# Sixteen batched matmuls on one core: from eight loads and turns of four stores to nine loads, eight stores, seven loads, eight stores

## The chip, the cores and the metric

The kernel runs on one core of a Trainium2 chip. The metric is device time in microseconds (us) of one execution; the time given is the median of several runs. One further execution was profiled, and all rows of the profile come from it.

## The reference

For each of 16 batches, x (768 x 512) transposed times y (768 x 1024), all in float32:

```python
batch, m, k, n = 16, 512, 768, 1024
# x: (batch, k, m), y: (batch, k, n)
np.einsum('bkm,bkn->bmn', x, y).astype(np.float32)
```

The inputs are drawn from a normal distribution. A batch reads 1.5 MB of x and 3 MB of y and writes 2 MB.

## The kernel before

Batches are the unit of everything. A batch b is loaded as float32 into `xs[b % 2]` and `ys[b % 2]` (one DMA for x, one for y), cast to bfloat16 by VectorE (DVE) into half b % 2 of `xb` and `yb`, multiplied by TensorE (PE), copied from PSUM by ScalarE (ACT) into `ob[b % 5]`, and stored by one DMA. There are NO = 5 output buffers `ob`.

PE works through a batch in two groups g of 48 / 2 = 24 matmuls each: a group is two of the four row blocks `mo` and fills one half of PSUM, `ps[g]`. It waits for a token of `room` before each group (L152); ACT returns a token after each copy (L176). So PE can be at most two groups ahead of the copies. PE counts finished groups in `groups` (L162), two per batch. Before a batch it waits for the casts (`ready`, L148, passed on from `cast` by GpSimd).

ACT takes the batches in order. Before batch b's copies, for b of 5 and up, it waits until the store that last used the buffer, of batch b - 5, has landed (`so`, L170).

DVE casts x of batch b after PE has finished batch b - 2 (L129: `groups` at least 2(b - 1)) and x has landed, then y when y has landed. The last batch's y is cast in two parts.

All DMAs, loads and stores, are issued by one engine, SyncE (SP), in the order of its program, into one queue. Each issue first waits on SP:

- `load(b)` (L104): x of batch b waits until x of batch b - 2 has been cast, y until y of b - 2 has been cast, since they share a buffer.
- `store(b)` (L95): waits until batch b + 1 has left PE (`groups` at least 2(b + 2), L99), which implies that batch b's copies are done, since the last group of b + 1 needed their `room`. The stores of batches 14 and 15 wait for the copies themselves (`outs`).

An instruction of SP that waits holds back all that follow it. The order of the program is made at L113 to L120 from FIRST = 8 and TURN = 4: loads 0 to 7, stores 0 to 3, loads 8 to 11, stores 4 to 7, loads 12 to 15, stores 8 to 14. The store of batch 15 follows at L188, after SP has waited for the stores of batches 11 to 13 (L182) and for the other engines.

Of the kernel before, what the change touches and what calls it, by code (L numbers as in the profile page):

```python
# [3 lines left out]

# [2 lines left out]

# [8 lines left out]
def kernel(  # L16
# [11 lines left out]
    B, K, M = x.shape  # L28
# [9 lines left out]
    y_v = y.rearrange("b (p ko) n -> b p ko n", ko=KT)  # L38
    o_v = out.rearrange("b (p mo) n -> b p mo n", mo=MT)

    FIRST = 8
    TURN = 4
    NO = 5
    KH = KT // 2

# [24 lines left out]
    def wide_dma(key, dst, src, dram_rows, load):  # L70


        if key not in made:
            made[key] = nc.sync.dma_start(dst, src)
            return made[key]
        pat = mybir.BassSymbolicTensorAccessPattern
        widen = lambda a: a.rearrange("(q r) k m -> q (r k m)", r=dram_rows)
        plain = lambda a: a.rearrange("p k m -> p (k m)")
        s, d = (widen(src), plain(dst)) if load else (plain(src), widen(dst))
        return nc.sync.add_instruction(_copy.replace(  # L80
            made[key].ins, name=nc.get_next_instruction_name(),
            ins=(pat(ap=s.ap, dtype=s.dtype, bass_ap=s, is_dma=False),),
            outs=(pat(ap=d.ap, dtype=d.dtype, bass_ap=d, is_dma=False),),
            sync_info=None, ant_dge_precooked=False))


    def parts(b):
        return 2 if b in (15,) else 1
# [2 lines left out]
    nx = [sum(1 + parts(a) for a in range(b)) + 1 for b in range(B)]  # L91

    def store(b):  # L95


        if b < B - 2:
            nc.sync.wait_ge(groups, 2 * (b + 2))  # L99
        else:  # L100
            nc.sync.wait_ge(outs, b - (B - 3))
        nc.sync.dma_start(o_v[b], ob[b % NO][:]).then_inc(so[b % NO], 16)

    def load(b):  # L104
        i = b % 2
        if b >= 2:
            nc.sync.wait_ge(cast, nx[b - 2])
        wide_dma("x", xs[i][:], x_v[b], 4, True).then_inc(sx[i], 16)
        if b >= 2:
            nc.sync.wait_ge(cast, nx[b - 2] + parts(b - 2))  # L110
        wide_dma("y", ys[i][:], y_v[b], 2, True).then_inc(sy[i], 16)

    for b in range(B):  # L113
        load(b)
        if b + 1 >= FIRST and (b + 1 - FIRST) % TURN == 0:
            a = b + 1 - FIRST
            for c in range(a, a + TURN):
                store(c)
    for b in range(B - FIRST + TURN, B - 1):
        store(b)  # L120


    for _ in range(60):
# [95 lines left out]
```

## Time and profile before

| what | us |
|---|---|
| median of 3 runs (lowest to highest) | 260.62 (260.34 to 261.06) |
| the profiled execution's own time | 260.58 |
| its span, first to last record | 258.8 |
| PE busy, of the span | 181.6 (70%) |
| DVE busy | 82.0 (32%) |
| ACT busy | 60.9 (24%) |
| issue to landing, median: load of x / of y / store | 20.1 / 18.6 / 27.2 |

The page's second part cuts the span into 40 slices of 6.5 us; each digit is the busy share of a slice in tenths. Its third part gives for each DMA queue the packets, the MB and the time that the packets took, as a share of 16 DMA engines over the span. Its fifth part lists groups of instructions: line, engine and operation, output and input, count, then busy time, the mean in ns of one, and the engine's idle time just before them with what ended most of it. In the timeline a row gives start, duration, engine (SPq is SP's queue of DMA issues; its duration is the issue, not the transfer), line, operation, count, and in brackets the idle time before and what ended it.

PE ran in these stretches: 18.9 to 62.7, 62.9 to 73.4, 73.8 to 84.4, 99.2 to 123.0, 126.5 to 150.3, 162.6 to 185.5, 189.8 to 212.4 and 226.0 to 249.6 us.

### The profile page before, as it was taken

What the parts mean: (1) busy time and instruction counts of PE and PEld (TensorE: products, weight loads), DVE (VectorE), ACT (ScalarE), POOL (GpSimd) and SP (SyncE); (2) the same over time, 40 slices, a digit from 0 to 9 for tenths busy, and PEclk for the clock granted to TensorE, in tenths of its full rate; (3) what the DMA queues carried; (4) which work ended last, traced back from release to release, by engine and by line L of the source; (5) the groups of instructions that cost most, each with busy time, mean ns of one, the idle gap of its engine ahead of it and who ended that gap; (6) DMA issues with size and microseconds to landing.
All of it is one profiled execution on the core that took longest, in us unless ns stands there. A gap on an engine that the chain in (4) does not pass through costs nothing. (4 is left out here: it accounts for less than half of the span.)

```text
span 258.8 us, 2506 instructions
## 1 busy us (share of the span) xinstructions
PE 181.6 (70%) x768; PEld 89.3 (34%) x768; DVE 82.0 (32%) x33; ACT 60.9 (24%) x33; POOL 0.2 (0%) x4
## 2 busy tenths in 40 slices
PE   0009999999999006999499920899669980099950
PEld 0004555554545002454145500355325530035520
DVE  0261645527164350011734525002255262300000
ACT  1000442234220005222214002324402200413430
POOL 0000000000000000000000000000000000000000
PEclk9999999999999855899779985699979995569995
DMA  7999989899999999999999989999899999999987
GB/s 273 424 475 410 471 380 479 372 479 395 456 410 441 387 418 430 466 446 418 433 433 425 471 352 443 420 461 479 372 479 403 448 410 390 433 438 420 436 357 324
DMA packets 4514, 109.07 MB, mean 421 GB/s; under 512 B 768, under 2 KB 768, under 8 KB 768
## 3 DMA queue, kind: packets, MB, share of 16 engines
q1 hardware_dynamic: 4512, 109.05, 98.6%
q14 instruction: 2, 0.02, 0.0%
HBM read 75.50 MB, written 33.55 MB: 421 GB/s over the span
## 5 line engine op out<-in xcount | busy, mean ns | idle before, releaser
L157 PE MATMUL ps<-yb,xb 128*128 x768 | 181.6, 402 | 68.0 <-PEq L152 68.0
L157 PEld LDWEIGHTS ps<-yb,xb 128*128 x768 | 89.3, 116 | 159.8 <-issue 89.8
L173 ACT COPY ob<-ps 128x2048 f32<-128x2048 f32 x32 | 59.6, 1872 | 185.3 <-PE ps L157 125.2
L135 DVE CAST yb<-ys 128x6144 bf16<-128x6144 f32 (+1 forms) x17 | 53.8, 3172 | 77.8 <-DMA ys<-in_y_dram 77.8
L131 DVE CAST xb<-xs 128x3072 bf16<-128x3072 f32 x16 | 28.2, 1761 | 62.5 <-DMA xs<-in_x_dram 48.7
L173 ACT ACT_TABLE_LOAD x1 | 1.3, 1283 | 5.3 <-issue 5.3
L203 POOL MEMSET const-bfloat16-1.0<- 128x1 bf16 x1 | 0.1, 103 | 0.0
L203 POOL MEMSET const-uint8-127<- 128x1 uint8 x1 | 0.1, 102 | 0.0
L203 POOL MEMSET const-float32-0.0<- 128x1 f32 x1 | 0.1, 100 | 0.2 <-issue 0.2
L203 POOL MEMSET const-float32-1.0<- 128x1 f32 x1 | 0.1, 99 | 0.0
## 6 DMA issues: line engine op xcount, KB each, us to landing
ys<-in_y_dram SPq DMA_DIRECT2D x16, 3072.0 KB, 18.6
out_dram<-ob SPq DMA_DIRECT2D x16, 2048.0 KB, 27.2
xs<-in_x_dram SPq DMA_DIRECT2D x16, 1536.0 KB, 20.1
```

The source lines that it names most:

```text
L131: nc.vector.tensor_copy(xb[:, i], xs[i][:]).then_inc(cast, 1)
L135: nc.vector.tensor_copy(yb[:, i, ks], ys[i][:, ks]).then_inc(cast, 1)
L157: mm = nc.tensor.matmul(ps[g][:, m, nt], x_w[:, bass.ds(s, 1), kt, mo], yb[:, bass.ds(s, 1), kt, nt * NF:(nt + 1) * NF], start=(kt == 0), ...
L173: cp = nc.scalar.copy(ob[b % NO][:, g * HB:(g + 1) * HB].rearrange("p m (t f) -> p m t f", f=NF), ps[g][:])
L203: nc = _bacc.Bacc("TRN2", target_bir_lowering=False, num_devices=1)
```

## The change

The two constants and the loop that made SP's order are replaced by a list of turns, each a number of loads and a number of stores. The order is now: loads 0 to 8, stores 0 to 7, loads 9 to 15, stores 8 to 14 (the last turn asks for eight stores; seven remain, and the store of batch 15 is issued at the end as before). `load`, `store`, their waits, the five output buffers and all other engines' programs are unchanged.

```diff
-    FIRST = 8
-    TURN = 4
+    TURNS = [(9, 8), (7, 8)]
     NO = 5
...
-    for b in range(B):
-        load(b)
-        if b + 1 >= FIRST and (b + 1 - FIRST) % TURN == 0:
-            a = b + 1 - FIRST
-            for c in range(a, a + TURN):
-                store(c)
-    for b in range(B - FIRST + TURN, B - 1):
-        store(b)
+    loads, stores = iter(range(B)), iter(range(B - 1))
+    for nl, ns in TURNS:
+        for b in islice(loads, nl):
+            load(b)
+        for b in islice(stores, ns):
+            store(b)
```

More of the change, by code (lines that the diff above doesn't have):

```diff
@@ L6 @@
 from contextlib import ExitStack
+from itertools import islice
 import concourse.bass as bass
```

## The prediction

> **What bounds the kernel now.** I read the page first: parts 2 and 3 for which resource is full, part 5 for who waits.
>
> ```profile
> DMA  7999989899999999999999989999899999999987
> q1 hardware_dynamic: 4512, 109.05, 98.6%
> L157 PE MATMUL ps<-yb,xb 128*128 x768 | 181.6, 402 | 68.0 <-PEq L152 68.0
> L173 ACT COPY ob<-ps 128x2048 f32<-128x2048 f32 x32 | 59.6, 1872 | 185.3 <-PE ps L157 125.2
> ```
>
> The one DMA queue is busy 98.6% of the span, PE 70%, ACT 24%. So the transfers set the time, and PE's 68.0 us of waiting for `room` cost nothing so long as the queue has something to move. [...] So next I read the timeline, where a cast begins when its load has landed and a copy that waited for an output buffer begins when that store has landed.
>
> ```profile
> 69.96 3.36 DVE L135 CAST yb<-ys 128x6144 bf16<-128x6144 f32 x1 [5.48 <-DMA ys<-in_y_dram]
> 73.71 1.76 DVE L131 CAST xb<-xs 128x3072 bf16<-128x3072 f32 x1 [0.39 <-DMA xs<-in_x_dram]
> 80.94 3.36 DVE L135 CAST yb<-ys 128x6144 bf16<-128x6144 f32 x1 [5.47 <-DMA ys<-in_y_dram]
> ...
> 92.12 3.36 DVE L135 CAST yb<-ys 128x6144 bf16<-128x6144 f32 x1 [5.66 <-DMA ys<-in_y_dram]
> ...
> 97.00 3.64 ACT L173 COPY ob<-ps 128x2048 f32<-128x2048 f32 x2 [21.69 <-DMA out_dram<-ob]
> ...
> 99.19 23.85 PE L157 MATMUL ps<-yb,xb 128*128 x96 [14.79 <-PEq L152]
> ...
> 107.59 1.87 ACT L173 COPY ob<-ps 128x2048 f32<-128x2048 f32 x1 [6.95 <-PE ps L157]
> 112.71 1.87 ACT L173 COPY ob<-ps 128x2048 f32<-128x2048 f32 x1 [3.26 <-PE ps L157]
> 115.34 1.76 DVE L131 CAST xb<-xs 128x3072 bf16<-128x3072 f32 x1 [19.86 <-DMA xs<-in_x_dram]
> 117.95 1.87 ACT L173 COPY ob<-ps 128x2048 f32<-128x2048 f32 x1 [3.37 <-PE ps L157]
> 123.07 1.87 ACT L173 COPY ob<-ps 128x2048 f32<-128x2048 f32 x1 [3.26 <-PE ps L157]
> ```
>
> Three things are to be seen. A load of one batch takes 10.98 us (y of batch 5 at 69.96, of 6 at 80.94), its x part 3.75 (69.96 to 73.71). The transfers land in the order of issue: y of batch 7 at 92.12, store 0 at 97.00 (4.88 later), then stores 1 to 3 and x of batch 8 by 115.34; 18.34 less 3.75 is three stores, 4.86 each. The same reading after y of batch 11 (copies at 160.43, cast at 178.65) gives 4.82; I use 4.84. And the first copy of batch 5 waits for store 0, because buffer 0 of five is still full; PE, with both PSUM halves occupied, stands still until it comes.
>
> The chain of waits names the end, and the timeline what precedes it:
>
> ```profile
> 218.85 3.43 DVE L135 CAST yb<-ys 128x3072 bf16<-128x3072 f32 x2 [4.69 <-DMA ys<-in_y_dram]
> 223.74 3.63 ACT L173 COPY ob<-ps 128x2048 f32<-128x2048 f32 x2 [19.83 <-DMA out_dram<-ob]
> 225.98 23.60 PE L157 MATMUL ps<-yb,xb 128*128 x96 [13.61 <-PEq L152]
> 249.61 1.87 ACT L173 COPY ob<-ps 128x2048 f32<-128x2048 f32 x1 [3.26 <-PE ps L157]
> 251.67 0.33 SPq L188 DMA_DIRECT2D out_dram<-ob  x1
> ```
>
> Store 8 lands at 223.74 and frees batch 13's copies; then come batches 14 and 15 on PE, the last copy, the last store. That is 35.1 us from store 8's landing to the end of the span, with all other stores beside it.
>
> [...] This trace: the last store, issued when the queue was all but empty, took 6.3 us to landing (the minimum of the landing times), 1.5 over the 4.84 of a store in a full queue; I use 6.3. [...] Here the first group of matmuls after a pause takes 8.40, 8.41, 7.41, 7.15 and 8.15 us (PE's start to the first copy after it), a later one 5.12 or 5.24.
>
> **The change part by part.**
>
> *Up to y of batch 7* nothing differs: the same loads, waits and landings.
>
> *Load 8 ahead of store 0.* It waits for the casts of batch 6, as before, so it is in the queue in time (those casts end at 75.5 and 84.3, while y of batch 7 is under way to 92). Its 10.98 us are moved, not added: y of batch 8 lands at 80.94 + 2 x 10.98 = 102.9, and store 0 at 107.8 instead of 97.0. PE idles 10.8 us longer after batch 5 (from 84.4); in itself that is free.
>
> *Stores 0 to 7 in one run.* Store b waits on SP until batch b+1 has left PE (L99). Stores 0 to 4 need batch 5, done at 84.4: they are issued at once. Stores 5, 6 and 7 need batches 6, 7 and 8, which PE can't begin before store 0 has landed. Before, store 7 had no such trouble: its four stores came after load 11 with batch 8 done at 140.0, and y of batch 11 landed at 155.5, so the queue was full. Now count from store 0's landing at 107.8, with the steps of the trace:
> - copies of batch 5 begin, PE restarts 2.18 later (97.00 to 99.18 there);
> - batch 6 takes 7.90 (mean of the five first groups) + 5.12, done at +15.2; batch 7 5.24 + 5.12, done at +25.6; batch 8 likewise, done at +35.9. Batch 8's casts begin when batch 6 is done and take 5.2, so they lie beside batch 7's 10.4; without that cover batch 8 would come later.
> - The queue moves stores 1 to 5 by +24.2 (5 x 4.84). Store 5 is issued at +15.2, in time.
> - Store 6 is issued at +25.6, lands 6.3 later at +31.9; in a full queue it would land at +29.0. Lost: 2.8.
> - Store 7 is issued at +35.9, lands at +42.2, where 7 x 4.84 = 33.9 would be the full queue. Lost: 8.3 in all, so 5.5 more.
>
> Nothing else can use these gaps: loads 9 to 15 stand behind store 7 in SP's own order, though their buffers are long free.
>
> *Loads 9 to 15* follow store 7 back to back: load 9 needs casts of batch 7, load 10 those of batch 8 (done near 128, store 7 issued at 143.7). PE restarts after y of batch 9, and at 10.4 a batch against 10.98 for a load it keeps up; copies of batches 9 to 12 need stores 4 to 7, landed. I cost this stretch at nothing beyond the shift. The bytes and transfers before y of batch 15 are the same 16 loads and 8 stores, so it lands 8.3 later: 227.2.
>
> *The end* is as before: batch 13's copies wait for store 8, and the 35.1 us follow.
>
> *Two turns fewer* from stores back to loads and on again: a first store after a load takes 4.88 against 4.84, so two turns are worth about 0.1 gained, and I drop it.
>
> **Sum.** 8.3 us on the profiled execution's own 260.58 (span 258.8, 1.8 around it), which is the median of the runs (260.62) but for 0.04: 268.9 us.
>
> Unknown sizes, bounded from both sides: the first group after a pause, 7.15 to 8.41, moves the gap by -0.8 to +0.5; the same ramp recurs at the end, where 8.15 is in the 260.58, so -1.0 to +0.3 there. A restart from an empty queue: at least the 0.9 between the last issue (251.67) and the first bytes after it, in windows of half a microsecond, at most the 2.5 of the first load (issued 0.95, cast at 7.18, less 3.75), against my 1.5: -0.6 to +1.0. These rarely all go one way: 267.5 to 270.5.
>
> **The rivals.**
>
> *Longer stop (chance 8%).* PE's pause is now some 26 us instead of 15[...]. For: [...] the queue's restart price rests on one store. Against: five restarts in the trace all lie within 1.3 us, after pauses of 3.4 to 14.8, and the very first group of the kernel, cold, took 7.5. It would give 270.5 to 273; with a clock that stays at half through batches 6 to 8, some 20 us more, which I hold for 1%.
>
> *Partly hidden (chance 5%).* the gap ahead of store 6 closes, because PE comes back sooner than I say or the stores drain more slowly, so that only store 7's remains: 8.3 - 2.8 = 5.5, 266.1. Against: store 6's wait for batch 7 follows from rates that repeat within 0.1.
>
> *Not slower (chance 3%).* One mechanism: the turns between reading and writing. The old order has five of them, the new three. If a turn cost 4.2 us or more, two fewer would pay for the gap: 260.6, and below it beyond that. The place to see it is the first transfer after each turn; there 4.88 stands against 4.84, and x of batch 8 and 12 show no loss either. That leaves the price near 0.05, and this rival nearly nothing to live on but a turn cost hidden in my averages.
>
> *The change not done:* the order of SP's instructions shows load 9 (batch 8) ahead of eight stores and seven loads behind them; nothing else moves. No chance left for it.
>
> **How the numbers follow.** Forecast 84%, longer stop 8%, partly hidden 5%, not slower 3%. The likeliest: 268.9. The range 267.4 to 270.8 holds the forecast's case and the near edge of the longer stop, leaving out somewhat under 2 in 10. All but the last case are slower by over 0.3% (0.8 us, about what a measurement of this kernel can tell from no change): slower 0.97, within 0.3% 0.01, faster 0.02.
>
> **What would show it.** In the profile after: copies of batch 5 near 107.8; PE without a pause over batches 6 to 8 (144 matmuls from about 110); stores issued singly near 123, 133.4 and 143.7; the DMA row with a dip between 131 and 146 and nowhere else; x of batch 9 cast near 153.7; y of batch 15 near 227.2; SP's waits on PE longer by the ones on stores 5 to 7. It is wrong if store 7 is issued before about 136 (then there is no gap), if the queue stays full between 131 and 146, or if a second gap opens among loads 9 to 15.

## The result and the profile after

| | before | after |
|---|---|---|
| median, us (lowest to highest) | 260.53 (260.34 to 261.06, 4 runs) | 269.90 (269.74 to 270.49, 4 runs) |
| profiled execution: time / span | 260.58 / 258.8 | 270.49 / 268.7 |
| share of the one DMA queue | 98.6% | 95.4% |

The ratio after to before is 1.0361, with a 95% interval of 1.0338 to 1.0383: 9.4 us slower. The profiled execution of after was the longest of its four, so its own difference is 9.9.

The page of the changed kernel, parts 2, 3 and 5:

```profile
DMA  7999999999999998999474999989989989999996
q1 hardware_dynamic: 4512, 109.05, 95.4%
L154 PE MATMUL ps<-yb,xb 128*128 x768 | 175.9, 393 | 82.2 <-PEq L149 82.2
```

The bytes are the same and the queue's share has fallen by 3.2 points of a longer span. The missing share lies in one place: slices 20 to 22 of the row, 4, 7 and 4 tenths. A slice is 6.7 us, so this is 127 to 148 us. PE idles more in total (82.2 us against 68.0), but that is no proof of anything, since it idled before without harm.

The timeline of the changed kernel at the run of eight stores and after it (start, duration, engine, line, what; SPq is the issue on SP; the three single stores are numbers 5, 6 and 7; ... stands for rows left out):

```profile
107.85 3.64 ACT L170 COPY ob<-ps 128x2048 f32<-128x2048 f32 x2 [32.49 <-DMA out_dram<-ob]
110.03 34.15 PE L154 MATMUL ps<-yb,xb 128*128 x144 [25.59 <-PEq L149]
...
118.38 1.87 ACT L170 COPY ob<-ps 128x2048 f32<-128x2048 f32 x1 [6.89 <-PE ps L154]
123.50 0.33 SPq L101 DMA_DIRECT2D out_dram<-ob  x1
...
133.85 0.33 SPq L101 DMA_DIRECT2D out_dram<-ob  x1
...
144.22 0.33 SPq L101 DMA_DIRECT2D out_dram<-ob  x1
144.59 0.48 SPq L74 DMA_DIRECT2D xs<-in_x_dram  x1
...
155.27 1.76 DVE L128 CAST xb<-xs 128x3072 bf16<-128x3072 f32 x1 [26.74 <-DMA xs<-in_x_dram]
...
228.47 3.43 DVE L132 CAST yb<-ys 128x3072 bf16<-128x3072 f32 x2 [5.49 <-DMA ys<-in_y_dram]
```

Store 0's landing releases ACT at 107.85; PE follows 2.18 us later and runs batches 6, 7 and 8 without a pause. At the end of each of them one store is issued: 123.50, 133.85, 144.22. Load 9 follows only 0.37 us after store 7, though the casts that it waits for, those of batch 7, had ended by 95.4 (y's began at 92.00 and took 3.36): SP issued in the order of its program, and store 7's wait held the load. What the queue does meanwhile is in a table by stretch of the same kernel (length; busy time of PE, of PE's weight loads, of DVE, ACT and GpSimd, each with its count of instructions; in the last three columns PE's clock, the DMA engines' mean share and GB/s; the share can pass 1: it is 1.24 at 145 to 146):

```profile
125.00:130.00 5.00, 5.00 (x25) 2.61 (x24) 3.53 (x2) 1.64 (x2) 0.00 (x0) 1.00 1.00 426
131.00:134.00 3.00, 3.00 (x16) 1.59 (x14) 0.00 (x0) 0.14 (x1) 0.00 (x0) 1.00 0.01 5
135.00:139.00 4.00, 4.00 (x20) 2.11 (x19) 0.00 (x0) 0.73 (x1) 0.00 (x0) 1.00 0.94 397
140.00:145.00 5.00, 4.18 (x20) 1.96 (x18) 0.00 (x0) 1.75 (x2) 0.00 (x0) 1.00 0.00 0
```

The waits of SP on PE, in the view of who waited for whom (total, times, longest), before and after:

```profile
SPq L102 <- PE ps L157: 37.2, 4, 26.5
```

```profile
SPq L101 <- PE ps L154: 91.0, 5, 36.1
```

PE is busy through both empty stretches, 131 to 134 and 140 to 145 (in the second up to the end of batch 8 at 144.2): here it is the engine that everything waits for. Outside them the queue is full again, and y of batch 15 lands 9.6 us later than before (228.47 against 218.85).

The end of the changed kernel, in the timeline:

```profile
233.30 3.63 ACT L170 COPY ob<-ps 128x2048 f32<-128x2048 f32 x2 [21.36 <-DMA out_dram<-ob]
...
242.58 1.87 ACT L170 COPY ob<-ps 128x2048 f32<-128x2048 f32 x1 [5.65 <-PE ps L154]
...
258.06 1.87 ACT L170 COPY ob<-ps 128x2048 f32<-128x2048 f32 x1 [3.26 <-PE ps L154]
260.12 0.33 SPq L185 DMA_DIRECT2D out_dram<-ob  x1
```

From store 8's landing to the end of the span it is 35.4 us (268.7 - 233.30), before 35.1. So all of the loss but 0.3 us is made by 155 us and is only carried along from there.

### The profile page after: what moved, and what is told of

It reads as the page before. It is cut to its first block, busy times and chain, and to the rows that moved or that the text cites. A ratio compares the mean times of both kernels' runs of the same rounds, so it can differ in the third digit from the quotient of the medians.

```text
span 268.7 us, 2506 instructions
## 1 busy us (share of the span) xinstructions
PE 175.9 (65%) x768; PEld 88.3 (33%) x768; DVE 81.9 (30%) x33; ACT 61.0 (23%) x33; POOL 0.2 (0%) x4
## 3 DMA queue, kind: packets, MB, share of 16 engines
q1 hardware_dynamic: 4512, 109.05, 95.4%
## 5 line engine op out<-in xcount | busy, mean ns | idle before, releaser
L154 PE MATMUL ps<-yb,xb 128*128 x768 | 175.9, 393 | 82.2 <-PEq L149 82.2
L154 PEld LDWEIGHTS ps<-yb,xb 128*128 x768 | 88.3, 115 | 169.2 <-issue 96.4
```

The source lines that it names most:

```text
L154: mm = nc.tensor.matmul(ps[g][:, m, nt], x_w[:, bass.ds(s, 1), kt, mo], yb[:, bass.ds(s, 1), kt, nt * NF:(nt + 1) * NF], start=(kt == 0), ...
```

## The experiments

Four theories were set against each other. A: the queue runs empty because stores 6 and 7 wait for batches 7 and 8 on PE, and these stand behind store 0. B: eight stores in a row, or the turns between reading and writing, cost time in themselves. C: PE is late and the end follows PE, whatever the queue does. D: it is the length of PE's pause, through a slower first group after it. Each kernel was timed against the kernel before on the same chip.

| run | us, median | ratio to before (95%) |
|---|---|---|
| e1: stores wait for copies | 261.85 | 1.0049 (1.0033 to 1.0066) |
| e2: load 9 ahead of stores 6 and 7 | 260.76 | 1.0002 (0.9993 to 1.0010) |
| e3: six output buffers | 260.40 | 0.9988 (0.9981 to 0.9995) |
| e4: one store after each load | 261.99 | 1.0052 (1.0037 to 1.0067) |
| e5: load 9 waits for store 7 | 271.04 | 1.0410 (1.0387 to 1.0432) |
| e6: ten loads, eight stores | 269.54 | 1.0332 (1.0315 to 1.0349) |
| e7: stores from load 5 on | 261.94 | 1.0060 (1.0047 to 1.0074) |
| e8: e1 and e2 together | 260.77 | 1.0004 (0.9996 to 1.0013) |
| e9: kernel before, six buffers | 260.68 | 1.0001 (0.9992 to 1.0010) |

**e1: the wait alone.** The order of the change stays; a store waits for its own batch's copies.

```diff
-        if b < B - 2:
-            nc.sync.wait_ge(groups, 2 * (b + 2))
-        else:
-            nc.sync.wait_ge(outs, b - (B - 3))
+        nc.sync.wait_ge(outs, b + 1)
...
-        if b == B - 2:
+        if b < B - 1:
             nc.scalar.drain().then_inc(outs, 1)
```

> The order of the change is kept, but store b waits for the copies of batch b (a count by ACT after each batch) and no longer for batch b+1 to leave PE. Theory A (the queue runs empty because stores 6 and 7 wait for batches 7 and 8 on PE, which stand behind store 0): counted from store 0's landing, the copies of batch 6 end at +17 and those of batch 7 at +28, so store 6 is issued in time and store 7 lands at 34 to 35 where a full queue gives 33.9: 260.5 to 261.7 us. Theory B (eight stores in a row are slow in themselves, or the turns cost): the run of eight is still there, so about 269.9 us.

261.85: the run of eight stores is still there and eight of the 9.4 us are gone, which B can't explain. It is 0.15 beyond A's upper figure, and that was followed up in e8.

**e2: the order alone.** Waits and buffers of the change; load 9 is put ahead of the two stores that come late.

```diff
-    TURNS = [(9, 8), (7, 8)]
+    TURNS = [(9, 6), (1, 2), (6, 7)]
```

> Loads 0 to 8, stores 0 to 5, load 9, stores 6 and 7, loads 10 to 15, the rest. Waits as in the change. Theory A: load 9 needs nothing that is late, and its 11.0 us fill the two gaps of 2.7 and 5.3 us; store 7 is issued 36 us after store 0's landing, when the queue has work until +40: 260.2 to 261.2 us. If instead PE's late return is a cost whatever the queue does (theory C: the batches after store 0 are late and the end follows PE), about 269 us.

260.76. In its timeline the load goes out right behind store 5, and store 7 is issued as late as in the change:

```profile
122.82 0.33 SPq L101 DMA_DIRECT2D out_dram<-ob  x1
123.20 0.90 SPq L74 DMA_DIRECT2D xs<-in_x_dram  x1
...
143.54 0.34 SPq L101 DMA_DIRECT2D out_dram<-ob  x1
```

PE finishes batch 8 at 143.5, only 0.7 us sooner than in the change (144.2), and nothing is lost. That takes away C: PE's lateness cost only what the queue lacked. It also shows what the change took away, which is work for the queue that needs nothing late.

**e3: the buffer alone.** Order and waits of the change, one output buffer more.

```diff
-    NO = 5
+    NO = 6
```

> The change with six output buffers instead of five. Theory A: batch 5's copies wait for nothing, batch 6 runs on PE before store 0 has landed, and batches 7 and 8 are done at +15 and +26 after it; store 7 lands by +33, ahead of 33.9: no gap, 259.8 to 260.8 us. Theory B: 269 us or more, since the order of transfers is the same.

260.40, the fastest of all. PE's timeline in e3, and the issue of store 7:

```profile
84.80 10.55 PE L154 MATMUL ps<-yb,xb 128*128 x48 [0.45 <-PEq L149]
109.94 22.39 PE L154 MATMUL ps<-yb,xb 128*128 x96 [14.59 <-PEq L149]
...
132.36 0.33 SPq L101 DMA_DIRECT2D out_dram<-ob  x1
```

Batch 6 now runs at 84.80, before store 0 has landed; only 96 matmuls are left after it instead of 144, and store 7 leaves 11.9 us earlier (132.36 against 144.22). The same order of transfers then has no gap: 98.8% on the page. This rules B out as the cause of the 9.4 us.

**e6: a longer pause.** One more load goes ahead of the eight stores.

```diff
-    TURNS = [(9, 8), (7, 8)]
+    TURNS = [(10, 8), (6, 7)]
```

> Ten loads, eight stores, six loads, the rest. Theory A: everything from store 0 on comes 11.0 us later, the gap in the run of stores keeps its size (2.7 and 5.3 us without packets), since PE still starts batch 6 from store 0's landing; only the place of load 9 differs: 269.3 to 270.6 us. Theory D (the loss comes from how long PE stood still, with its colder restart): 11 us more of standing makes it longer than 270.6 us.

269.54. The page's row of DMA shares in e6, and then PE's timeline in e6:

```profile
DMA  7999999999999999999995389989989989999996
```

```profile
120.97 43.78 PE L154 MATMUL ps<-yb,xb 128*128 x192 [36.58 <-PEq L149]
```

The dip has moved by 11 us, and in place of two empty stretches of 3.0 and 5.3 us there are two of 2.3 and 5.3 (142.6 to 144.9 and 150.0 to 155.3). PE's pause is 36.6 us instead of 25.6 and its batch 6 takes 12.7 us against 13.5. So the length of the pause is not the cause, and D is out. The slow restart as such stays a part of the loss: the first group took 8.35 us in the change and a later one 5.12, so some 3 us of batch 8's lateness are its doing (an estimate from these two times).

**e5: why store 7 took longer than store 6.** In the change store 6, alone in the queue, landed 6.3 us after its issue (133.85 to 140.19) and store 7 7.3 after its own (144.22 to 151.49). Here load 9 is held back until store 7 has landed.

```diff
         for b in islice(loads, nl):
+            if b == 9:
+                nc.sync.wait_ge(so[7 % NO], 32)
             load(b)
```

> The change, with load 9 held on SP until store 7 has landed. In the change store 7 took 7.3 us from issue to landing and store 6, alone in the queue, 6.3. If the extra 1.0 us comes from the loads queued right behind it, store 7 takes 6.3 to 6.4 here, and load 9's x lands 5.2 to 6.2 after that: 270.5 to 272 us. If it is store 7's own, it takes 7.3 again, and the time is 271.5 to 273 us.

The timeline of e5 has store 7's issue, and load 9 at its landing:

```profile
142.45 0.33 SPq L101 DMA_DIRECT2D out_dram<-ob  x1
...
148.75 0.48 SPq L74 DMA_DIRECT2D xs<-in_x_dram  x1
149.28 0.59 SPq L74 DMA_DIRECT2D ys<-in_y_dram  x1
```

Store 7 was issued at 142.45 and landed at 148.74: 6.3 us. In e6, where loads stand right behind store 7 again, it took 7.3 (154.42 to 161.69). So the extra microsecond goes with the loads queued right behind it. Holding them back doesn't pay: load 9's x lands 12.6 us after batch 8 has left PE (10.96 in the change), and the time is 1.1 longer.

**e8: what was left in e1.** The edits of e1 and e2 together.

> Stores wait for the copies, as in e1, and load 9 stands ahead of stores 6 and 7, as in e2. e1 was 1.2 us slower than the kernel before. If that is store 7 still coming into the queue at the last moment (issued 134.95, with the packets of store 6 ending within a microsecond or two), it goes here: 260.4 to 261.1 us. If it is ACT's counting after each batch, it stays: 261.6 to 262.2 us.

260.77 against 260.64 for the kernel before: ACT's counting costs nothing that can be measured. So e1's 1.2 us come with store 7's late issue. The timeline of e1:

```profile
134.95 0.33 SPq L98 DMA_DIRECT2D out_dram<-ob  x1
135.33 0.48 SPq L74 DMA_DIRECT2D xs<-in_x_dram  x1
135.85 1.35 SPq L74 DMA_DIRECT2D ys<-in_y_dram  x1
...
146.96 1.76 DVE L125 CAST xb<-xs 128x3072 bf16<-128x3072 f32 x1 [19.26 <-DMA xs<-in_x_dram]
```

There store 7 leaves at 134.95 and lands at 142.23, again 7.3 us, where a full queue would have it at 107.97 + 33.9 = 141.9; and x of batch 9 follows it by 4.6 us instead of 3.7. In e3, with the same order and the issue 2.6 us earlier, x of batch 9 follows by 3.6. Store 7 of e1 was issued 2.1 us before store 6 landed, that of e3 4.5 us before. So time is lost in a queue that is all but empty, though in e1 no stretch of over a quarter of a microsecond is without packets. What the queue does in that time stays open.

**e4 and e7: the price of turns.** One store after each load, from load 7 or from load 5 on: 17 and 21 turns, where the kernel before has 5.

```diff
-    TURNS = [(9, 8), (7, 8)]
+    TURNS = [(8, 1)] + [(1, 1)] * 8 + [(0, 6)]
```

> Loads 0 to 7, then store 0, load 8, store 1, load 9 and so on to load 15, store 8, the rest: 17 turns between reading and writing, where the kernel before has 5 and the change 3. If a turn costs nothing that the landings show (my figure was 0.05 us), 260.3 to 261.3 us, as the kernel before. If a turn had a price hidden in the averages, of 0.5 us say, 266 us.

```diff
-    TURNS = [(9, 8), (7, 8)]
+    TURNS = [(6, 1)] + [(1, 1)] * 10 + [(0, 4)]
```

> Loads 0 to 5, then one store after each further load, so that 5 stores and the last one stand after load 15's first store. No wait is left that comes later than its place in the queue: the end no longer hangs on store 8, batches 14 and 15, and the last copy, but on the queue. 16 loads of 10.98 and 16 stores of 4.85 follow each other without a gap: 259.8 to 260.5 us, 0.1 to 0.7 less than the kernel before, if turns cost nothing.

Both expectations missed: 261.99 and 261.94, slower than before. Over 12 turns more e4 loses 1.36 us, over 16 more e7 loses 1.31 (both against 260.63 for the kernel before, timed with them): about 0.1 us a turn. In neither is the queue without packets for over a quarter of a microsecond, so this is not the loss of the change. It is an average: the four turns that e7 has more than e4 cost nothing further, so a fixed price for each turn isn't shown. e7 was meant to beat both kernels, and lost more than it could gain.

**e9: where e3's last 0.3 us come from.** The kernel before with `NO = 6`.

> The kernel before (eight loads, turns of four stores) with six output buffers. e3, the changed order with six, is 0.3 us under the kernel before. If that comes from the end (batch 13's copies no longer wait for store 8, so the last store finds a full queue), it is here too: 260.1 to 260.6 us. If it comes from two turns fewer, 260.6 to 260.8 us, as before.

260.68, as the kernel before (260.64). So the sixth buffer by itself gains nothing, and e3's gain goes with its order. Two turns fewer at about 0.1 each would fit e4 and e7, but this is the edge of what can be measured and isn't shown.

## Why the prediction was right

It gave 268.9 (267.4 to 270.8); 269.90 was measured. By its steps:

- *The long run of stores is gated by PE, and PE by store 0.* Shown: e3 cuts the second link, e1 loosens the first, and with either most of the loss is gone; e2 leaves both and fills the gap.
- *Store 0 at 107.8.* It landed at 107.82, and the copies that it released began at 107.85.
- *Batches 6, 7 and 8 done at +15.2, +25.6, +35.9.* Measured from the issues: +15.65, +26.0, +36.4. The term that was off by 0.45 is the first group after the pause: 8.35 us (110.03 to 118.38) where I put the mean of five, 7.90. It lies inside the bounds of 7.15 to 8.41, but these were too narrow. In the five restarts of the kernel before, the granted clock of PE was 0.50 for 6.0, 6.0, 4.0, 3.4 and 5.5 us (99.19 to 105.19 in the first of them), and these groups took 8.40, 8.41, 7.41, 7.15 and 8.15. In the change it was 0.50 for 5.9 us after the restart (110.03 to 115.92); in e5, after the same pause of 25.59 us, PE ran at half clock for 2.9 us (109.77 to 112.62), and there the group took 6.84. The length of the pause alone doesn't set this stretch: it was 6.0 us after a pause of 14.79 and after one of 3.44. What sets it was not shown.
- *Store 6 lost 2.8, store 7 8.3.* Measured: store 6 landed 3.3 us after its place in a full queue, store 7 9.8 after it (151.49 against 107.82 + 33.9). Besides the 0.45 the mis-sized term is store 7's issue to landing: 7.3, not the 6.3 of a store that is alone. My price was read from the last store of the kernel, which has nothing behind it; e5 shows that this is the difference. The bound of 1.0 upwards for the restart was what held it, and that was luck: it was read from the kernel's first load, not from a store with loads behind it.
- *Loads 9 to 15 back to back, no second gap.* So it was: y of batch 15 came 73.2 us after x of batch 9 (228.47 - 155.27); six loads of 10.98 and one y of 7.23 (10.98 less 3.75) make 73.1.
- *The end as before.* The sum is right (35.4 against 35.1), but not the way. PE's first group there took 7.05 us instead of 8.15, and the last copy was over 26.6 us after store 8's landing instead of 27.7. The last store went out 1.1 sooner by that count and gained nothing: it landed 7.8 us after its issue instead of 6.3, behind stores 13 and 14. Here the queue closed the kernel, not PE, and I had not seen that the two were that close. e9 says the same of the order of before: with six buffers its last store was issued at 249.15, 9.1 us ahead of its landing, so the end no longer hung on PE, and the time stayed (260.68 against 260.64). So the path that I gave for the 35.1 us was wrong; the sum held because the queue's path was as long.
- *Two turns dropped at 0.1.* Half of what e4 and e7 say, 0.1 a turn and 0.2 for two; too little to matter here. But their loss without a gap shows that a change of order can cost time where it leaves the queue no gap, and the forecast had counted only gaps. The rival that lived on a price of 4.2 us a turn is shown to be empty.
- *The longer stop.* It was right in one thing, the slow restart of the queue, with 1.0 us; its clock that stays low was not: the granted clock was 1.00 from 115.92 to the end of batch 8 at 144.2, and e6, with the longest pause, has the shorter batch 6. Its 20 us were also too low: at a granted clock of 0.50 PE did 14 matmuls in 5.88 us, so the 144 of batches 6 to 8 would take about 60 us where the forecast had 33.7 (an estimate).
- *Partly hidden.* It did not come: the queue stood empty for 3.0 us ahead of store 6.

The sum by measured terms for the profiled execution: 8.3 + 0.45 + 1.0 = 9.8 at store 7, 9.6 at y of batch 15, 9.9 at the end.

## What to carry to other kernels

When one queue is the bound, ask of every transfer in it which engine's result its issue waits for, and which earlier transfer of the same queue that engine needs; if the answer comes back to the same run of transfers, the buffers decide how long the run can be: here eight stores in a row ran dry with five buffers and the waits of the change (269.90 us), and not with six buffers (260.40). Count in landings from the first transfer of the run, and keep some transfer that waits for nothing late behind each one that does. Issue a transfer well ahead of its turn: here a store issued 2.1 us before the landing of the one ahead of it came with a loss of over a microsecond without a visible gap (e1), and one issued 4.5 us before it lost nothing (e3).

## What the runs showed of the hardware

- A 2 MB store issued into an empty queue landed after 6.3 us with nothing queued behind it and after 7.3 us with loads behind it (e5 against the change and e6). In the full queue of the change stores 0 to 4 landed 4.84 apart (107.82 to 127.19). In the change the issues of the loads behind it also took 1.33 to 1.36 us each on SP from the second on; 0.59 in e5, and 0.47 where a load was issued on its own into a full queue. That came without an empty queue too: in e3, whose queue never ran dry, the loads issued right behind store 7 took 1.11 to 1.14 us. Whether the long issues and the late landing are one thing was not tried.
- Many turns between reading and writing cost 1.3 to 1.4 us here, about 0.1 each on average, and not on all of the 16 parts in which the trace shows a transfer to land alike. In e4 the first part of y of batch 15 lands at 217.50 and the last at 220.23, in the kernel before at 217.43 and 218.83: the first parts lose nothing, the last fall behind. The transfer right after a turn (4.88 against 4.84) hardly shows it; the one ahead of the turn does. In e4, for batches 9 to 14, y with a store behind it lands 7.43 to 7.72 us after its x, where it was 7.30 to 7.31 in the kernel before. Which parts these are, and why, stays open.
